# Attention, gate and branch pools that wait by tile, laid out from two ends of SBUF

## The chip, the cores and the metric

The kernel runs on one core of a Trainium2 chip. The metric is the time on the device in microseconds. Before the change three runs took 956.02, 958.73 and 959.63 us, the median is 958.73 us.

## What is computed

One decoder block over 1024 tokens of width 1024, all in fp32:

```python
h = rms_norm(x, g_pre[l], NORM_EPS)
proj = jnp.einsum('bsd,dn->bsn', h, w_in[l])
qa, ka, va, fa, za, qb, kb, vb, zb, gates = jnp.split(proj, SPLIT_POINTS, axis=-1)
log_f = jax.nn.log_sigmoid((fa + b_forget[l]).astype(jnp.float32)).transpose(0, 2, 1)
ya = fox_attention(split_heads(qa, FOX_HEADS), split_heads(ka, FOX_HEADS),
                   split_heads(va, FOX_HEADS), log_f)
ya = merge_heads(ya) * jax.nn.silu(za)
...
yb = diff_attention(qd, kd, vd, lam)
yb = rms_norm(yb, g_subln[l], SUBLN_EPS) * (1.0 - lam_init)
yb = merge_heads(yb) * jax.nn.silu(zb)
gate_a, gate_b = jnp.split(jax.nn.sigmoid(gates), N_BRANCHES, axis=-1)
merged = (gate_a * jnp.einsum('bsw,wd->bsd', ya, w_branch[l, 0])
          + gate_b * jnp.einsum('bsw,wd->bsd', yb, w_branch[l, 1]))
y = jnp.einsum('bsd,de->bse', merged, w_out[l])
x = x + rms_norm(y, g_post[l], NORM_EPS)
```

`fox_attention` is causal softmax attention of eight heads of 64, with the running sum of `log_f` added to the scores. `diff_attention` takes the difference of two causal softmaxes for each of four heads, `softmax(q1 k1) - lam * softmax(q2 k2)`, and its q and k go through rope first.

## The kernel before, in words

Every fp32 product is made of three products of a high and a low part (hi·hi, hi·lo, lo·hi). So a weight block is loaded (`raw`), its high part cast (`hi`) and its low part subtracted (`lo`); all three tiles come from `wpool`, two buffers each, in all stages.

The stages follow one another, each in pools of its own, and the bytes of a closed pool are used again by pools opened later:

1. The V stage (L119–222) normalizes x, transposes it into `hT` and projects the values of both attentions, token block by token block (`pv`, L195). The results are spilled to DRAM (`vb_d` L203, `va_d` L211).
2. Attention (L251–645) has eight units u: 0 to 3 are the heads of the differential attention, 4 to 7 pairs of heads of the other. `unit_proj` projects keys (`pk`) and queries (`pq`) in two halves c of 24 matmuls each (`project`, L246). For u below 4 each half goes through `rope` (L280): ACT copies it out of PSUM (L283), four DMAs on the SP queue swap its rows (`sw`, L287), DVE and POOL multiply by cosine and sine (L288, L289), DVE adds (L290), and `stack` makes the parts TA, TB, KA and KB (L295–298). `unit_attn` loads the unit's values (`V`, L495), builds swapped copies `X0`/`X1` of the queries by DMA (L407), and works row by row: scores (`S`, L421 and L422), their minimum on DVE (L423), exponential on ACT (L428), transposes (L450) and products with V (L474), evacuation to `y_d` (L523, L555). The projections of the next unit, of the z columns (`pz`, spilled to `z_d`) and the combinations of `hT` (`t_d`, L373) are fillers between rows. Pools: `qk` (TA, TB, KA, KB, X, V), `pp` (score rows P and small work tiles such as the lambda inputs `lt`, L570), `ptp`, `stg`, and in PSUM `pj`, `sps`, `tps2`, `yps`. `big`, opened before the V stage, holds the tables and later `cb` and is closed at L647.
3. The gates (L654–821). `h_load` (L790) loads the combined right operands T6, T5, T7, T4 from `t_d`, two tiles of 1 MB each, into `tpool`. `gates_plain(0)` makes the first gate block with 96 plain matmuls (`pg`, L246). `gates_pair(d)`, d from 1 to 7, makes the others by Winograd's form with seven products (`x1` to `x7`, L713): the two weight blocks `raw{d}_0`, `raw{d}_1` are loaded (L802), POOL makes the sums S1 to S4 (L677), ACT and DVE or POOL split them (`a1` to `a7`, L664, L665), DVE combines the products (`c`, L706), ACT applies the sigmoid (L775) and the gate is spilled (`g_d`, L776). `y_load` brings back the attention results (`yd0`, `yd1`, later `yf2`, `yf3`), `y_work` multiplies them by the z gates. Pools: `wx`, `tmp`, `ydp`, `tpool`, and `xps` in PSUM.
4. The branches (L824–873) work in `mpool` (`mg`, and `e0` to `e3`) over the bytes of `tpool`; the output projection follows.

A scheduler places the instructions of each engine by its own estimate of times, within the dependences, so the order on an engine is not that of the code. All DMAs named here are issued by one queue, SP, in its order; each uses one of eight semaphores in turn and waits for the DMA eight places before it.

By default a pool opened over released bytes makes its tiles wait for all users of every released pool there. With `reuse_waits="tile"` a tile waits for the users of those earlier tiles that lay on its own bytes (or in its own PSUM bank). With `side="right"` a pool is laid out from the upper end of SBUF downwards, otherwise from the lower end upwards.

Of the kernel before, what the change touches and what calls it, by code (L numbers as in the profile page):

```python
# [10 lines left out]
F32R = mybir.dt.float32r  # L11
AF = mybir.ActivationFunctionType
ALU = mybir.AluOpType
PSUM = bass.MemoryType.PSUM
DRAM = bass.MemoryType.DRAM

P = 128
# [4 lines left out]
CH = 512  # L22
# [19 lines left out]
def f32(ap):  # L42
    return ap.bitcast(F32)
# [3 lines left out]
def tile_hybrid_block(  # L47
# [18 lines left out]
    nc = tc.nc  # L66
# [41 lines left out]
    t_d = {m: [dram.tile([P, 4, CH], F32, name=f"t_d{m}_{part}") for part in range(2)]  # L108
           for m in (4, 5, 6, 7)}
# [9 lines left out]
    with ExitStack() as st:  # L119
        vw = st.enter_context(tc.tile_pool(name="vw", bufs=1))  # L120
        xp = st.enter_context(tc.tile_pool(name="xp", bufs=2))
        tps = st.enter_context(tc.tile_pool(name="tps", bufs=2, space=PSUM))
# [126 lines left out]


    with ExitStack() as st:  # L251
        qk = st.enter_context(tc.tile_pool(name="qk", bufs=2))
        pp = st.enter_context(tc.tile_pool(name="pp", bufs=6))
        ptp = st.enter_context(tc.tile_pool(name="ptp", bufs=3))
        stg = st.enter_context(tc.tile_pool(name="stg", bufs=2))
        pj = st.enter_context(tc.tile_pool(name="pj", bufs=2, space=PSUM))
        sps = st.enter_context(tc.tile_pool(name="sps", bufs=3, space=PSUM))
        tps = st.enter_context(tc.tile_pool(name="tps2", bufs=2, space=PSUM))
        yps = st.enter_context(tc.tile_pool(name="yps", bufs=1, space=PSUM))

        nc.sync.dma_start(gsub, g_subln.rearrange("o p -> p o"))
        nc.gpsimd.tensor_scalar(gsub, gsub, 1.0 - LAM_INIT, 1.0, op0=ALU.mult, op1=ALU.mult)
# [351 lines left out]
        T, tasks = unit_proj(0)  # L614
# [3 lines left out]
        for u in range(8):  # L618
# [5 lines left out]
            if u + 1 < 8:  # L624
                T, tasks = unit_proj(u + 1)
# [26 lines left out]


    gw = ExitStack()  # L654
    wx = gw.enter_context(tc.tile_pool(name="wx", bufs=2))
    tmp = gw.enter_context(tc.tile_pool(name="tmp", bufs=8))
    ydp = gw.enter_context(tc.tile_pool(name="ydp", bufs=1))
    xst = ExitStack()
    xps = xst.enter_context(tc.tile_pool(name="xps", bufs=8, space=PSUM))

    def split(dst, src, eng=nc.vector):

# [82 lines left out]


    tst = ExitStack()
    tpool = tst.enter_context(tc.tile_pool(name="tpool", bufs=1))

    yz = {}  # L750

# [26 lines left out]
    def gates_plain(d):  # L778
        for br in range(2):
            wt = load_w(f"g{br}_{d}", w_cols(GT + br * D + d * P), True, True)  # L780
            for c in range(2):
# [5 lines left out]
    h_ops = {m: [[hT[part][kh][sh][:, k, :] for k in range(4)] for part in range(2)]  # L787
             for m, (kh, sh) in hB.items()}

    def h_load():  # L790
        for m in (6, 5, 7, 4):
            ts = [tpool.tile([P, 4, CH], F32R, tag=f"T{m}{part}", name=f"T{m}{part}")
                  for part in range(2)]
            for part in range(2):
                nc.sync.dma_start(f32(ts[part]), t_d[m][part])
            h_ops[m] = [[t[:, k, :] for k in range(4)] for t in ts]

    def gates_pair(d, order):
        raw = []
# [8 lines left out]

    ORD = (1, 6, 5, 7, 2, 3, 4)
    h_load()  # L810
    gates_plain(0)
    for t in range(4):
# [8 lines left out]
    tst.close()  # L821


    mpool = gw.enter_context(tc.tile_pool(name="mpool", bufs=1))  # L824
    mg = mpool.tile([P, KT, S], F32, name="mg")
    hslot = {(kh, sh): [(hpool, f"h{part}{kh}{sh}") for part in range(2)]
             for kh in range(2) for sh in range(2)}
# [187 lines left out]
```

## Time and profile before

| what | us |
|---|---|
| median of three runs | 958.73 |
| the profiled execution | 960.13 |
| span of its trace | 958.0 |
| TensorE (PE) busy in the span | 900.7 |
| VectorE (DVE) busy | 627.2 |
| ScalarE (ACT) busy | 437.0 |
| GpSimd (POOL) busy | 489.6 |
| last matmul of the V stage begins | 110.26 |
| last matmul of attention begins | 602.05 |

A row of the timeline reads: start, duration, engine, line, operation, result<-inputs, shape and count, and in brackets how long the engine had idled before and what ended that. SPq are the issues of the DMA queue SP. A row of the windows lists for a stretch of time the busy time and count of PE, PEld (weight loads of TensorE), DVE, ACT and POOL, then the granted clock of TensorE as a share of full speed, the share of the DMA engines and the GB/s. Names leave numbers out: `swk` is the swapped half of a key chunk, whichever.

### The profile page before, as it was taken

To read this page: it belongs to the slowest core of one execution; us is meant where nothing else is said; L and a number is where in the kernel's file an instruction comes from. 1 tells how busy PE (TensorE), PEld (TensorE's weight loads), DVE (VectorE), ACT (ScalarE), POOL (GpSimd) and SP (SyncE) were. 2 spreads that over 40 slices of the span, in tenths; PEclk is the share of its full clock that TensorE was granted. 3 is DMA by queue.
4 is the path that set the end of the run, shared out by engine and by line. 5 is a ranking of instruction groups with operands and counts; after the bars stand their busy time and mean duration, and the time that the engine had idled before them with its cause. 6 is when DMAs were issued, how large, how long until landed. Compare 5 with 4: busy or idle time off the path is not lost.

```text
span 958.0 us, 13760 instructions
## 1 busy us (share of the span) xinstructions
PE 900.7 (94%) x4600; PEld 752.1 (79%) x4600; DVE 627.2 (65%) x1180; ACT 437.0 (46%) x862; POOL 489.6 (51%) x460
## 2 busy tenths in 40 slices
PE   7999989899999999999999988999999999999992
PEld 5999867787887888888878877777888768887871
DVE  7731258978768868578676478228665782559875
ACT  3521125665656574565745658323443550324331
POOL 7200035446545466464644575216655735878972
PEclk9999999999999999999999999998999989999997
DMA  9532454434334353534434350893445696210144
GB/s 314 193 110 91 142 134 114 105 80 123 97 94 138 95 155 116 154 122 130 143 123 136 103 186 28 325 377 122 139 138 172 186 370 203 73 38 1 48 150 154
DMA packets 115656, 136.95 MB, mean 143 GB/s; under 512 B 10609, under 2 KB 80241, under 8 KB 114562
## 3 DMA queue, kind: packets, MB, share of 16 engines
q1 hardware_dynamic: 115586, 136.08, 44.4%
q8 instruction: 36, 0.59, 0.3%
q14 instruction: 34, 0.28, 0.1%
HBM read 85.65 MB, written 37.81 MB: 129 GB/s over the span
## 4 chain that ended last, share of the span: by engine, by line
PE 58%; DVE 13%; POOL 8%; DMA 7%; issue 6%; ACT 5%; SPq 2%; DVEq 0%; POOLq 0%; ACTq 0%
PE x_g L713 11%; PE pv L195 9%; PE pb L848 9%; PE pz L246 7%; PE pk L246 4%; PE pq L246 3%; PE ypf L474 3%; PE pg L246 2%; PE ptf L450 2%; DMA swk<-rawk 2%; SPq L287 1%; DVE Pd L423 1%; PE ypd L474 1%; PE Sf L421 1%; DVE wo_op L890 1%
## 5 line engine op out<-in xcount | busy, mean ns | idle before, releaser
L195 PE MATMUL pv<-wvhi,hT 128*128 128x264 f32 (+2 forms) x384 | 89.3, 325 | 0.4 <-DVE hT L181 0.4
L246 PE MATMUL pk<-hT,hi_k 128*128 128x512 f32 x256 | 83.9, 401 | 4.2 <-DVE KB L298 2.4
L246 PE MATMUL pz<-hT,hi_z 128*128 128x512 f32 x256 | 85.1, 400 | 0.0
L848 PE MATMUL pb<-yT,hi_br 128*128 128x512 f32 x256 | 80.8, 398 | 1.9 <-ACT hi_br L232 1.6
L246 PE MATMUL pq<-hT,hi_q 128*128 128x512 f32 x256 | 82.3, 395 | 0.0
L713 PE MATMUL x_g<-T,a_g 128*128 128x512 f32 x336 | 79.5, 392 | 1.6 <-ACT a_g L664 1.2
L713 PE MATMUL x_o<-wo_op,a_o 128*128 128x512 f32 x336 | 77.4, 391 | 2.4 <-ACT a_o L664 1.2
L713 PEld LDWEIGHTS x_o<-wo_op,a_o 128*128 128x128 f32 x336 | 62.8, 188 | 16.9 <-ACT a_o L664 2.1
L713 PEld LDWEIGHTS x_g<-T,a_g 128*128 128x128 f32 x336 | 63.5, 190 | 15.7 <-ACT a_g L664 1.6
L195 PEld LDWEIGHTS pv<-wvhi,hT 128*128 128x128 f32 x384 | 64.6, 190 | 6.2 <-DVE hT L181 0.7
L542 POOL TENSOR_SCALAR Pf<-Pf,lf 128x1024 f32<-128x1024 f32 (+3 forms) x64 | 52.5, 824 | 30.2 <-DVE lf L430 27.4
L713 PE MATMUL x_g<-hT,a_g 128*128 128x512 f32 x252 | 62.0, 400 | 2.6 <-ACT a_g L664 2.0
L428 ACT ACTIVATE Pf<-Pf,mxf 128x1024 f32<-128x1024 f32 (+3 forms) x64 | 49.8, 778 | 32.1 <-DVE mxf L423 29.5
L428 ACT ACTIVATE Pd<-Pd,mxd 128x128 f32<-128x128 f32 (+7 forms) x64 | 49.5, 774 | 30.0 <-DVE mxd L423 28.2
L538 POOL TENSOR_TENSOR cb<-cb,trim 128x128 f32<-128x128 f32 x64 | 30.0, 470 | 62.9 <-DVE mxf L423 45.1
L195 PE MATMUL pv<-wvlo,hT 128*128 128x512 f32 (+2 forms) x192 | 61.9, 325 | 0.0
L512 POOL TENSOR_SCALAR Pd<-Pd,ld 128x128 f32<-128x128 f32 (+7 forms) x32 | 25.6, 799 | 68.8 <-DVE ld L511 38.2
L848 PEld LDWEIGHTS pb<-yT,hi_br 128*128 128x128 f32 x256 | 49.1, 193 | 13.1 <-ACT hi_br L232 2.0
L713 PEld LDWEIGHTS x_g<-hT,a_g 128*128 128x128 f32 x252 | 48.5, 193 | 13.7 <-ACT a_g L664 2.4
L246 PEld LDWEIGHTS pk<-hT,hi_k 128*128 128x128 f32 x256 | 47.6, 190 | 14.4 <-DVE KB L298 2.5
L454 DVE TENSOR_TENSOR plf<-ptf,phf 128x512 fp32r<-128x512 f32 (+1 forms) x80 | 49.6, 633 | 10.1 <-ACT phf L453 9.5
L246 PEld LDWEIGHTS pz<-hT,hi_z 128*128 128x128 f32 x256 | 47.9, 191 | 8.7
(243 smaller groups left out, 2426.6 us busy)
## 6 DMA issues: line engine op xcount, KB each, us to landing
t_d<-t SPq DMA_DIRECT2D x32, 256.0 KB, 2.2
T<-t_d SPq DMA_DIRECT2D x8, 1024.0 KB, 14.9
raw<-in_w_in_dram SPq DMA_DIRECT2D x14, 512.0 KB, 4.1
g_d<-c_g SPq DMA_DIRECT2D x21, 256.0 KB, 3.9
vb_d<-vbs SPq DMA_DIRECT2D x8, 512.0 KB
va_d<-vas SPq DMA_DIRECT2D x8, 512.0 KB, 3.8
raw_k<-in_w_in_dram SPq DMA_DIRECT2D x8, 512.0 KB, 5.3
raw_q<-in_w_in_dram SPq DMA_DIRECT2D x8, 512.0 KB
```

The costliest lines, as they stand in the source:

```text
L195: nc.tensor.matmul(ps[n], lhsT=hT[hp][k // 4][i // 4][:, k % 4, hs], rhs=wt[k][:, a:b], start=first, stop=(k == KT - 1 and hp == 1))
L246: nc.tensor.matmul(ps, lhsT=a[:, k, :], rhs=hT[h][k // 4][c][:, k % 4, :], start=(k == 0 and a is hi and h == 0), stop=(k == KT - 1 and a ...
L287: nc.sync.dma_start(sw[b * 32:(b + 1) * 32, :], raw[o * 32:(o + 1) * 32, :])
L428: nc.scalar.activation(pr[:, 0:n], pr[:, 0:n], AF.Exp, bias=mx[:, len(pcs) - 1:len(pcs)], scale=-1.0, accum_out=le)
L450: nc.tensor.transpose(pt[:, o * P:(o + 1) * P], rows[2 * g + r][:, j * P:(j + 1) * P], ident)
L454: nc.vector.tensor_tensor(pl[:, 0:n], pt[:, 0:n], ph[:, 0:n], op=ALU.subtract)
L474: nc.tensor.matmul(o, lhsT=a, rhs=b[:, src], start=(j == 0 and n == 0), stop=(odd == 1 and jj == g and n == len(prods) - 1))
L512: nc.gpsimd.tensor_scalar(p2[:, 0:n], p2[:, 0:n], l2, 1.0, op0=ALU.mult, op1=ALU.mult)
L538: nc.gpsimd.tensor_tensor(diag, diag, trim, op=ALU.add)
L542: nc.gpsimd.tensor_scalar(p1[:, 0:n], p1[:, 0:n], l1, 1.0, op0=ALU.mult, op1=ALU.mult)
L713: nc.tensor.matmul(x[m], lhsT=a[:, ai, k, :], rhs=right[m][bi][k], start=(k == 0 and n == 0), stop=(k == 3 and n == 2))
L848: nc.tensor.matmul(ps, lhsT=a[:, kk, :], rhs=yT[g][h][:, k % 2, sl], start=(k == 0 and a is hi and h == 0), stop=(k == 3 and a is lo))
```

## The change

All SBUF and PSUM pools of attention, gates and branches get `reuse_waits="tile"`. `pp`, `ptp` and `stg` of attention and `wx`, `tmp` and `ydp` of the gates move to the right end. In `h_load` all eight T tiles are made ahead of their loads, in the order 6, 4, 7, 5; the loads keep their order 6, 5, 7, 4. `wpool` is not changed. In the new layout the T tiles lie over `big` and `qk` of attention: T6 over `cb` of unit 7 and over TA of unit 6, T4 and T7 over the operands of units 6 and 7, T5 over V and X. Before, `tpool` lay over V, X, `pp`, `ptp` and `stg`.

```diff
-        qk = st.enter_context(tc.tile_pool(name="qk", bufs=2))
-        pp = st.enter_context(tc.tile_pool(name="pp", bufs=6))
-        ptp = st.enter_context(tc.tile_pool(name="ptp", bufs=3))
-        stg = st.enter_context(tc.tile_pool(name="stg", bufs=2))
-        pj = st.enter_context(tc.tile_pool(name="pj", bufs=2, space=PSUM))
...
+        qk = st.enter_context(tc.tile_pool(name="qk", bufs=2, reuse_waits="tile"))
+        pp = st.enter_context(tc.tile_pool(name="pp", bufs=6, side="right", reuse_waits="tile"))
+        ptp = st.enter_context(tc.tile_pool(name="ptp", bufs=3, side="right", reuse_waits="tile"))
+        stg = st.enter_context(tc.tile_pool(name="stg", bufs=2, side="right", reuse_waits="tile"))
+        pj = st.enter_context(tc.tile_pool(name="pj", bufs=2, space=PSUM, reuse_waits="tile"))
...
-    wx = gw.enter_context(tc.tile_pool(name="wx", bufs=2))
-    tmp = gw.enter_context(tc.tile_pool(name="tmp", bufs=8))
-    ydp = gw.enter_context(tc.tile_pool(name="ydp", bufs=1))
+    wx = gw.enter_context(tc.tile_pool(name="wx", bufs=2, side="right", reuse_waits="tile"))
+    tmp = gw.enter_context(tc.tile_pool(name="tmp", bufs=8, side="right", reuse_waits="tile"))
+    ydp = gw.enter_context(tc.tile_pool(name="ydp", bufs=1, side="right", reuse_waits="tile"))
...
-    xps = xst.enter_context(tc.tile_pool(name="xps", bufs=8, space=PSUM))
+    xps = xst.enter_context(tc.tile_pool(name="xps", bufs=8, space=PSUM, reuse_waits="tile"))
...
-    tpool = tst.enter_context(tc.tile_pool(name="tpool", bufs=1))
+    tpool = tst.enter_context(tc.tile_pool(name="tpool", bufs=1, reuse_waits="tile"))
...
     def h_load():
+
+        ts = {m: [tpool.tile([P, 4, CH], F32R, tag=f"T{m}{part}", name=f"T{m}{part}")
+                  for part in range(2)] for m in (6, 4, 7, 5)}
         for m in (6, 5, 7, 4):
-            ts = [tpool.tile([P, 4, CH], F32R, tag=f"T{m}{part}", name=f"T{m}{part}")
-                  for part in range(2)]
             for part in range(2):
-                nc.sync.dma_start(f32(ts[part]), t_d[m][part])
-            h_ops[m] = [[t[:, k, :] for k in range(4)] for t in ts]
+                nc.sync.dma_start(f32(ts[m][part]), t_d[m][part])
+            h_ops[m] = [[t[:, k, :] for k in range(4)] for t in ts[m]]
...
-    mpool = gw.enter_context(tc.tile_pool(name="mpool", bufs=1))
+    mpool = gw.enter_context(tc.tile_pool(name="mpool", bufs=1, reuse_waits="tile"))
```

The number of instructions on each engine stays; the order that the scheduler makes changes. On the SP queue at the start of attention, before (the names carry unit and half: `swk0_0` are the four swaps for the keys of unit 0, half 0; `va_d` and `vb_d` are the last spills of the V stage):

```order
50 L211 DMA va_d_97<-vas7_1116 128x1024
51 L572 DMA lt_1160<-in_lambda_q2_dram 128x64
52 L572 DMA lt_1160<-in_lambda_k2_dram 128x64
53 L495 DMA V0_1345<-vb_d_96 128x8x256
54 L495 DMA V1_1912<-vb_d_96 128x8x256
55 L228 DMA raw_q1_1514<-in_w_in_dram 128x8x128
56 L287 DMA swk0_0_1210<-rawk0_0_1208 32x512 x4
57 L287 DMA swq0_0_1255<-rawq0_0_1253 32x512 x4
58 L287 DMA swk0_1_1294<-rawk0_1_1292 32x512 x4
59 L407 DMA X0d0_0_1351<-TA0_1173 64x256 x2
60 L407 DMA X1d0_0_1354<-TB0_1174 64x256 x2
61 L287 DMA swq0_1_1333<-rawq0_1_1331 32x512 x4
```

The load of `raw_z0` follows three rows further down, as row 64. And after:

```order
50 L203 DMA vb_d_96<-vbs7_1112 128x1024
51 L228 DMA raw_k1_1401<-in_w_in_dram 128x8x128
52 L495 DMA V0_1345<-vb_d_96 128x8x256
53 L495 DMA V1_1912<-vb_d_96 128x8x256
54 L211 DMA va_d_97<-vas7_1116 128x1024
55 L287 DMA swk0_0_1210<-rawk0_0_1208 32x512 x4
56 L228 DMA raw_q1_1514<-in_w_in_dram 128x8x128
57 L228 DMA raw_z0_1850<-in_w_in_dram 128x8x128
58 L287 DMA swq0_0_1255<-rawq0_0_1253 32x512 x4
59 L287 DMA swk0_1_1294<-rawk0_1_1292 32x512 x4
60 L287 DMA swq0_1_1333<-rawq0_1_1331 32x512 x4
61 L407 DMA X0d0_0_1351<-TA0_1173 64x256 x2
```

The lambda loads `lt` have moved up among the earlier spills, V stands ahead of the last `va_d`, and `raw_z0` and all swaps of unit 0 stand ahead of its first X loads.

On PE, the rows around the first score of attention (`Sd0_0_0_0`), before (`pk1_0` are keys of unit 1) and after (`pq1_0` are its queries):

```order
698 L246 MATMUL pk1_0_1407<-hT100_92,hi_k1_1403 128x512
699 L246 MATMUL pk1_0_1407<-hT000_88,lo_k1_1404 128x512
700 L246 MATMUL pk1_0_1407<-hT000_88,hi_k1_1403 128x512
701 L421 MATMUL Sd0_0_0_0_1359<-KA0_1175,TA0_1173 128x128
702 L246 MATMUL pk1_0_1407<-hT100_92,hi_k1_1403 128x512
703 L246 MATMUL pk1_0_1407<-hT000_88,lo_k1_1404 128x512
704 L421 MATMUL Sd0_1_0_0_1368<-KB0_1176,TB0_1174 128x128
```

After:

```order
721 L246 MATMUL pq1_0_1520<-hT000_88,hi_q1_1516 128x512
722 L246 MATMUL pq1_0_1520<-hT100_92,hi_q1_1516 128x512
723 L246 MATMUL pq1_0_1520<-hT000_88,lo_q1_1517 128x512
724 L246 MATMUL pq1_0_1520<-hT000_88,hi_q1_1516 128x512
725 L421 MATMUL Sd0_0_0_0_1359<-KA0_1175,TA0_1173 128x128
726 L246 MATMUL pq1_0_1520<-hT100_92,hi_q1_1516 128x512
727 L421 MATMUL Sd0_1_0_0_1368<-KB0_1176,TB0_1174 128x128
728 L421 MATMUL Sd0_0_1_0_1381<-KA0_1175,TA0_1173 128x256
```

The first score has moved behind 24 more projection matmuls: before it follows 10 of `pk1_0`, after it follows all of `pk1_0` and 10 of `pq1_0`.

On the SP queue at the start of the gates, before (`T60` is the high part of T6, `ys7_0` an attention result of unit 7, `ox` a block of x for the output stage):

```order
289 L555 DMA y_d7_106<-ys7_2_6574 128x256
290 L555 DMA y_d7_106<-ys7_1_6759 128x256
291 L760 DMA yd0_7041<-y_d0_99 128x1024
292 L760 DMA yd0_7041<-y_d1_100 128x1024
293 L555 DMA y_d7_106<-ys7_0_6856 128x256
294 L760 DMA yd1_7044<-y_d2_101 128x1024
295 L760 DMA yd1_7044<-y_d3_102 128x1024
296 L931 DMA ox4_1_8960<-in_x_dram 128x512
297 L931 DMA ox5_1_8986<-in_x_dram 128x512
298 L795 DMA T60_6901<-t_d6_0_137 128x2048
299 L795 DMA T61_6902<-t_d6_1_138 128x2048
300 L795 DMA T50_6905<-t_d5_0_135 128x2048
```

After:

```order
293 L555 DMA y_d7_106<-ys7_1_6759 128x256
294 L796 DMA T60_6901<-t_d6_0_137 128x2048
295 L796 DMA T61_6902<-t_d6_1_138 128x2048
296 L796 DMA T50_6907<-t_d5_0_135 128x2048
297 L555 DMA y_d7_106<-ys7_0_6856 128x256
298 L796 DMA T51_6908<-t_d5_1_136 128x2048
299 L796 DMA T70_6905<-t_d7_0_139 128x2048
300 L796 DMA T71_6906<-t_d7_1_140 128x2048
301 L796 DMA T40_6903<-t_d4_0_133 128x2048
302 L796 DMA T41_6904<-t_d4_1_134 128x2048
303 L932 DMA ox4_1_8960<-in_x_dram 128x512
304 L932 DMA ox5_1_8986<-in_x_dram 128x512
```

The T loads stand ahead of the loads of `yd`, and three of them ahead of the last spill of attention.

On ACT at the end of gate pair 1, before (`a1_g2` is the first left operand of pair 2):

```order
538 L664 CAST a4_g1_7172<-raw1_1_7049 128x512
539 L775 ACTIVATE c22_g1_7128<-c22_g1_7128 128x512
540 L775 ACTIVATE c11_g1_7067<-c11_g1_7067 128x512
541 L775 ACTIVATE c12_g1_7107<-c12_g1_7107 128x512
542 L775 ACTIVATE cu2_g1_7089<-cu2_g1_7089 128x512
543 L664 CAST a1_g2_7203<-raw2_0_7199 128x512
544 L664 CAST a5_g2_7243<-S1_g2_7221 128x512
```

After:

```order
538 L664 CAST a4_g1_7172<-raw1_1_7049 128x512
539 L775 ACTIVATE c22_g1_7128<-c22_g1_7128 128x512
540 L775 ACTIVATE c11_g1_7067<-c11_g1_7067 128x512
541 L775 ACTIVATE c12_g1_7107<-c12_g1_7107 128x512
542 L664 CAST a1_g2_7203<-raw2_0_7199 128x512
543 L775 ACTIVATE cu2_g1_7089<-cu2_g1_7089 128x512
544 L664 CAST a5_g2_7243<-S1_g2_7221 128x512
```

The cast of `a1_g2` stands ahead of the sigmoid of `cu2_g1`. From gate pair 7 to the end the orders of all engines are the same in both.

More of the change, by code (lines that the diff above doesn't have):

```diff
@@ L251, in tile_hybrid_block @@
     with ExitStack() as st:
-        qk = st.enter_context(tc.tile_pool(name="qk", bufs=2))
-        pp = st.enter_context(tc.tile_pool(name="pp", bufs=6))
-        ptp = st.enter_context(tc.tile_pool(name="ptp", bufs=3))
-        stg = st.enter_context(tc.tile_pool(name="stg", bufs=2))
-        pj = st.enter_context(tc.tile_pool(name="pj", bufs=2, space=PSUM))
-        sps = st.enter_context(tc.tile_pool(name="sps", bufs=3, space=PSUM))
-        tps = st.enter_context(tc.tile_pool(name="tps2", bufs=2, space=PSUM))
-        yps = st.enter_context(tc.tile_pool(name="yps", bufs=1, space=PSUM))
+        qk = st.enter_context(tc.tile_pool(name="qk", bufs=2, reuse_waits="tile"))
[3 more added lines that the diff above has]
+        pj = st.enter_context(tc.tile_pool(name="pj", bufs=2, space=PSUM, reuse_waits="tile"))
+        sps = st.enter_context(tc.tile_pool(name="sps", bufs=3, space=PSUM, reuse_waits="tile"))
+        tps = st.enter_context(tc.tile_pool(name="tps2", bufs=2, space=PSUM, reuse_waits="tile"))
+        yps = st.enter_context(tc.tile_pool(name="yps", bufs=1, space=PSUM, reuse_waits="tile"))
         nc.sync.dma_start(gsub, g_subln.rearrange("o p -> p o"))
```

## The prediction

> **What bounds the kernel now.** First the page: how busy the engines are, then the slices, then the chain that ended last.
>
> ```profile
> PE 900.7 (94%) x4600; PEld 752.1 (79%) x4600; DVE 627.2 (65%) x1180; ACT 437.0 (46%) x862; POOL 489.6 (51%) x460
> PE   7999989899999999999999988999999999999992
> PE 58%; DVE 13%; POOL 8%; DMA 7%; issue 6%; ACT 5%; SPq 2%; DVEq 0%; POOLq 0%; ACTq 0%
> ```
>
> TensorE is busy 900.7 of 958.0 us, and no matmul is removed. A change of waits can therefore win only from the 57 us in which PE idles or runs at a low clock, and most of those lie where no pool changes: the slices of the first and the last 24 us stand at 7 and 2 tenths. So I looked at the two places where a pool is opened over bytes that were in use: the start of attention (110 us) and the start of the gates (602 us). How fast PE goes when nothing holds it, from the chain at the second place, and then the timeline of PE and the windows at the first:
>
> ```profile
> 603.23 22.07 PE pg L246 x96
> 110.39 0.63 PE L246 MATMUL pk<-hT,hi_k 128*128 128x512 f32 x2
> 117.10 0.50 PE L246 MATMUL pq<-hT,lo_q 128*128 128x512 f32 x1 [0.61 <-DVE lo_q L236]
> 134.99 0.70 PE L246 MATMUL pk<-hT,hi_k 128*128 128x512 f32 x2 [1.73 <-ACT rawk L283]
> 137.74 0.50 PE L246 MATMUL pk<-hT,lo_k 128*128 128x512 f32 x1 [2.04 <-DVE lo_k L236]
> 140.95 0.31 PE L421 MATMUL Sd<-KA,TA 128*128 128x128 f32 x1
> 132.00:136.00 4.00, 1.97 (x8) 1.02 (x6) 3.91 (x5) 1.82 (x3) 1.85 (x2) 1.00 0.00 0
> 136.00:140.00 4.00, 2.26 (x6) 1.83 (x7) 3.91 (x5) 1.82 (x3) 1.09 (x1) 0.78 0.33 82
> 168.00:200.00 32.00, 28.90 (x144) 24.43 (x145) 29.76 (x67) 19.44 (x35) 16.87 (x13) 0.95 0.42 111
> ```
>
> One 128x512 matmul costs 22.07/96 = 0.23 us. Attention opens with 96 projection matmuls of unit 0 and 10 of unit 1 before the first score at 140.95. Unbroken, 106 x 0.23 = 24.4 us after 110.39 would be 134.8; the first score is 6.2 us later than that. PE misses 4.00-1.97 and 4.00-2.26 = 3.8 us between 132 and 140, and the rest is a wait of 0.61 at 116.5 and a clock of 0.78. DVE is at 3.91 of 4 us in both windows. Why everything comes at once there is seen on the queues and in the first rows that rope gives:
>
> ```profile
> 110.58 0.33 SPq L572 DMA_DIRECT2D lt<-in_lambda_q_dram  x1
> 113.88 1.41 SPq L495 DMA_DIRECT2D V<-vb_d  x2
> 119.56 4.68 SPq L287 DMA_DIRECT2D swk<-rawk  x4
> 134.87 2.41 SPq L287 DMA_DIRECT2D swk<-rawk  x4
> 138.43 1.15 SPq L407 DMA_DIRECT2D X0d<-TA  x2
> 116.07 0.59 ACT L283 COPY rawk<-pk 128x512 f32<-128x512 f32 x1 [5.11 <-PE pk L246]
> 129.35 1.80 POOL L289 TENSOR_TENSOR swk<-swk,sinT 128x512 f32<-128x512 f32 x1 [19.12 <-DMA swk<-rawk]
> 132.37 1.48 POOL L234 TENSOR_SCALAR hi_k<-raw_k 128x1024 fp32r<-128x1024 f32 x1
> 136.47 1.22 DVE L236 TENSOR_TENSOR lo_k<-raw_k,hi_k 128x1024 fp32r<-128x1024 f32 x1
> 144.86 0.29 DVE L423 CUSTOM_DVE_ANT_0 Pd<-Sd,dmask 128x128 f32<-128x128 f32 x1
> 145.08 1.78 DVE L288 TENSOR_TENSOR rawq<-rawq,cosT 128x512 f32<-128x512 f32 x1
> ```
>
> The copy of the first projected chunk is there at 116.7 (116.07+0.59), yet its swap DMAs start at 119.56 and POOL has the swapped rows only at 129.35. Ahead of them on SP stand the four small lambda loads, which begin at 110.58, when the V stage's last reader of the bytes is done, and behind those the two loads of V at 113.88. POOL then does two rope products and only after them the high part of unit 1's key weights, so lo_k comes at 136.47 and PE stands.
>
> **Start of attention, part by part.** With waits by tile the lambda loads go out among the V stage's last spills, and the V loads no longer follow them. I put them at 109.2, behind the last vb_d and raw_k, 4.7 us earlier. Then the swaps are not held by the queue and leave at 116.7, when the copy is done: 119.56-116.7 = 2.9 us earlier. The two V loads in flight have also gone by then, so I take the landing 6 us earlier (at most 129.35 - 116.7 - 4.68 = 8, at least 2.9). hi_k of unit 1 now stands directly behind the first rope product on POOL and not behind the second. The rope product would start at 123.4 (129.35-6), and 1.80 for it, 1.48 for hi_k and 1.22 for lo_k make 127.9 for the end of lo_k, against 137.7 now. That is ahead of PE's need: by the new order pk of unit 1 begins after 96 matmuls, at 110.39 + 22.1 = 132.5. Both waits of PE, 1.73 and 2.04, then have nothing behind them.
>
> The order has 130 projection matmuls ahead of the first score where 106 stood: 110.39 + 130 x 0.23 = 140.3, plus at most the 0.6 at 116. The first score comes no earlier, but with 24 x 0.23 = 5.5 us of filler done. On DVE the whole rope of unit 0 is done before the first L423, where before the last chunk came after it: 1.78 for its cosine product and 3 x 0.69 for the add and the two subtractions of the stack:
>
> ```profile
> 134.42 0.69 DVE L296 TENSOR_TENSOR KA<-rawk,KA 64x512 fp32r<-64x512 f32 x1
> ```
>
> together 3.85 us. What is this lead worth? The filler would have had to be done anyway, so at most PE's lost 6.2. At the least it is the first row alone, about 1 us (144 instead of 144.86), if the filler was only needed where PE is idle anyway. I take 4: between 168 and 200 us DVE is busy 29.76 of 32 us and PE 28.90, so the smaller lead, DVE's 3.85, should be the one that survives. V, X and the score buffers cost nothing of their own: V is first needed by the products, well after 145.
>
> Moved past on SP, and priced: the load of z's weights, which has to wait for lo_k of unit 1 (it takes that raw buffer), stands ahead of three of the four swaps in the new order. With lo_k at 128 it holds them about as long as the copy of pq does (96 minus 24 matmuls: 110.39+16.6+0.6 = 127.6). So nothing, unless lo_k is late (a rival below). va_d's last spill goes behind V; unit 0's lo_q waits for its buffer, and the order has put pk's second chunk between, 24 x 0.23 = 5.5 us of cover; without it the wait of 0.6 us at 116 grows to some 2.
>
> **Start of the gates.**
>
> ```profile
> 602.05 0.28 PE L474 MATMUL ypf<-plf,V 128*128 128x128 f32 x1
> PE pg L246 <- DVE ys L552: 0.9, 1, 0.9
> 601.09 0.32 SPq L555 DMA_DIRECT2D y_d<-ys  x1
> 602.36 0.80 SPq L760 DMA_DIRECT2D yd<-y_d  x2
> 604.00:628.00 24.00, 24.00 (x107) 19.84 (x106) 4.01 (x5) 6.74 (x11) 5.24 (x4) 1.00 1.01 406
> 644.58 1.27 POOL L677 TENSOR_TENSOR S_g<-raw 128x512 f32<-128x512 f32 x1 [14.05 <-DMA raw<-in_w_in_dram]
> 645.11 0.63 ACT L775 ACTIVATE cu_g<-cu_g 128x512 f32<-128x512 f32 x1 [2.09 <-DVE cu_g L706]
> 645.64 0.60 ACT L664 CAST a_g<-raw 128x512 fp32r<-128x512 f32 x1
> 646.30 0.83 PE L713 MATMUL x_g<-hT,a_g 128*128 128x512 f32 x2 [1.95 <-ACT a_g L664]
> 647.82 4.63 PE L713 MATMUL x_g<-hT,a_g 128*128 128x512 f32 x10 [0.69 <-DVE a_g L665]
> 648.00:652.00 4.00, 4.00 (x10) 3.13 (x11) 4.00 (x4) 1.00 (x2) 3.37 (x3) 0.50 0.00 0
> ```
>
> The first gate matmul waits 0.9 us for the last copy out of the old banks; in the new program it has no wait. That 0.9 is the surest gain. The T loads go out behind the y_d spill of 601.09, some 1 us earlier than the yd loads that led the queue, but yd only moves behind T. Ahead of the second gate pair's weights stand the same bytes: T 8 MB, yd 2, ox 0.5, g_d 1, yf 2, together 13.5 MB at the window's 406 GB/s, 33 us of a full queue. So those weights land about 1 us earlier, no more. Their late landing (644.58) meets PE at the end of pair 1: idle 1.95+0.69 = 2.64 us, and then 10 matmuls take 4.63 where 10 x 0.23 and the last one's tail make 2.5, so 2.1 us go to the clock of 0.50. In the new ACT order the cast of a1 stands ahead of the cu activation that waited for DVE, so it can start when the first weight block has landed. I expect 1 to 1.7 us of the 2.64 to go, and the clock's 2.1 to go in about one case in three. The bounds are 0.9 and 0.9+2.64+2.1 = 5.6; I take 3.
>
> The rule that speaks to those 2.1 us: the Trainium skill ("TensorE: Matmul & The Clock Gate", "Why this matters for your kernels") asks for no PE-idle gap above about 3 us, one window of idle being what sets the clock back. By it two gaps of 1.95 and 0.69 would leave the clock alone; the row 648–652 disagrees with 0.50. By the rule the gate place would hold 3.5 us at most instead of 5.6.
>
> **The rest.** From the last gate pair on PE, ACT, DVE, POOL and SP stand in the same order as before, so the branch pool's new waits are priced at 0: the first mg load stands on SP behind the branch weights, the yT casts behind the last z work on ACT. T's landing under attention's old buffers costs nothing while T is first read 22 us into the gates, behind pg's 22.07 us.
>
> **Sum.** The profiled execution took 960.13 us, 1.4 above the median of the runs shown. 960.13 - 4 - 3 = 953.1; on the median's scale 951.7, so 952. A measurement of this kernel can tell about 0.5%, 4.8 us, from no change: faster is below 953.9, slower above 963.5.
>
> **Rivals.**
> - *Absorbed lead.* The filler done early leaves PE with less to put between the rows later. For it: PE is at 28.90 of 32 us from 168 to 200 with DVE at 29.76, so PE idles there for DVE. By the orders the lead of 24 to 30 matmuls is given back by unit 3 or 4. Or the change does not do what it says: something else than the old bytes (the copy, the queue's eighth DMA before) holds the swaps. Then 1 + 2 remain: 957.1, on the median's scale 956.
> - *Everything comes through.* 6.2 + 5.6 = 11.8: 948.3, on the median's scale 947. Against it: raw weights land only 1 us earlier.
> - *A new wait on SP* (slower). Unit 1's lo_k frees the buffer of z's weights, and that load now stands ahead of three swaps and the first X loads. If lo_k comes no earlier than now (it ends at 137.7), three swaps of 2.41 follow, X0d and X1d at 1.15 each and about 2 us of landing (as the t_d transfers' 2.2): X at 137.7 + 0.5 + 7.2 + 2.3 + 2 = 149.7, where the first X score runs at 143.2:
>
> ```profile
> 143.21 0.39 PE L422 MATMUL Sd<-KA,X0d 128*128 128x128 f32 x2
> 146.05 0.53 SPq L228 DMA_DIRECT2D raw_z<-in_w_in_dram  x1
> t_d<-t SPq DMA_DIRECT2D x32, 256.0 KB, 2.2
> ```
>
> 6.5 us later, and about 1.8 more for a clock near 0.5 after such a gap (as at 648). 960.13 + 8.3 - 3 = 965.4, on the median's scale 964. It decides from a lo_k later than about 130. Against it: hi_k was moved up on POOL, and V goes early.
>
> **Chances.** My forecast 0.42, the absorbed lead 0.30, everything 0.15, the new wait on SP 0.13. The forecast's own range is 949 to 955, from the bounds of each place. Leaving out the lower half of "everything" and most of the slow case gives 946 to 962 for 8 in 10. Faster by over 0.5%: 0.34 of the forecast's 0.42, 0.15, and 0.04 of the absorbed lead, 0.53. Slower: two thirds of the new wait and a little for places not seen, 0.11. Within: 0.36.
>
> **What would show it.** The swaps' first issue near 116.7 and POOL's first rope product near 123; no PE idle from 132 to 140; first score at 140 to 141, first L423 at 143 to 145; pg right behind the last attention matmul; PE idle before the second pair's first matmul 1.3 or less, and the clock at 648. If the last attention matmul is not about 4 us earlier than 602.05, the lead was absorbed. The prediction is wrong if the first L423 comes later than 146, if raw weights of pair 2 land later than 644.6, or if a slice after 200 us loses PE time that it had.

## The result and the profile after

Four runs of the changed kernel took 950.96 to 953.65 us, median 952.35; four of the kernel before 956.02 to 959.63, median 958.97. The ratio is 0.994, with a 95% interval from 0.9918 to 0.9962. The medians lie 6.6 us apart, and the forecast was 952. The profiled execution is the fastest of the four, 950.96 us, so it stands 9.2 us under the one before, and not 6.6.

First the page of the changed kernel, then the SP queue at the start of attention:

```profile
span 948.8 us, 13757 instructions
PE 896.9 (95%) x4600; PEld 747.2 (79%) x4600; DVE 627.2 (66%) x1180; ACT 437.2 (46%) x862; POOL 490.9 (52%) x460
```

```profile
109.69 1.00 SPq L495 DMA_DIRECT2D V<-vb_d  x2
112.02 1.29 SPq L211 DMA_DIRECT2D va_d<-vas  x1
117.26 2.52 SPq L287 DMA_DIRECT2D swk<-rawk  x4
...
128.81 0.38 SPq L228 DMA_DIRECT2D raw_z<-in_w_in_dram  x1
129.28 3.96 SPq L287 DMA_DIRECT2D swq<-rawq  x4
133.35 2.42 SPq L287 DMA_DIRECT2D swk<-rawk  x4
138.89 2.41 SPq L287 DMA_DIRECT2D swq<-rawq  x4
142.41 1.15 SPq L407 DMA_DIRECT2D X0d<-TA  x2
```

V leaves 4.2 us earlier than before and the first swaps, of keys, 2.3 us earlier. The first swaps of queries leave 5.0 us later (129.28, before 124.33). The second half's two leave 1.5 and 2.1 us earlier (133.35 and 138.89, before 134.87 and 140.96), but the first X loads, which now stand behind all of them, leave later: X0d at 142.41 where it left at 138.43. Now the other engines there (DVE, POOL, PE) and three windows:

```profile
121.77 1.23 DVE L236 TENSOR_TENSOR lo_q<-raw_q,hi_q 128x1024 fp32r<-128x1024 f32 x1 [9.70 <-DMA va_d<-vas]
127.55 1.23 DVE L236 TENSOR_TENSOR lo_k<-raw_k,hi_k 128x1024 fp32r<-128x1024 f32 x1
135.54 1.83 DVE L288 TENSOR_TENSOR rawq<-rawq,cosT 128x512 f32<-128x512 f32 x1 [6.04 <-DMA swq<-rawq]
149.09 0.29 DVE L423 CUSTOM_DVE_ANT_0 Pd<-Sd,dmask 128x128 f32<-128x128 f32 x1
```

```profile
122.61 1.54 POOL L289 TENSOR_TENSOR swk<-swk,sinT 128x512 f32<-128x512 f32 x1 [11.93 <-DMA swk<-rawk]
```

```profile
129.01 0.73 PE L246 MATMUL pq<-hT,hi_q 128*128 128x512 f32 x2 [0.68 <-ACT rawq L283]
141.72 0.50 PE L246 MATMUL pq<-hT,lo_q 128*128 128x512 f32 x1 [1.07 <-DVE lo_q L236]
143.67 0.22 PE L421 MATMUL Sd<-KA,TA 128*128 128x128 f32 x1
```

```profile
132.00:136.00 4.00, 4.00 (x20) 3.30 (x19) 0.46 (x1) 0.59 (x1) 0.46 (x1) 1.00 0.55 131
136.00:140.00 4.00, 4.00 (x19) 3.33 (x18) 3.90 (x3) 1.12 (x2) 3.98 (x3) 1.00 0.09 21
168.00:200.00 32.00, 31.15 (x165) 25.78 (x163) 24.44 (x63) 20.98 (x39) 17.66 (x14) 1.00 0.46 120
```

PE is busy without a gap from 132 to 140. The rows of attention, though, start at 149.09, 4.2 us later than before (144.86). And still attention ends earlier, as the last rows of PE in it and the first of the gates show:

```profile
597.92 0.27 PE L474 MATMUL ypf<-plf,V 128*128 128x128 f32 x1
598.03 0.68 PE L246 MATMUL pg<-hT,hi_g 128*128 128x512 f32 x2
```

From the first `pk` to the last `ypf` it took 491.66 us before (602.05-110.39) and 486.95 after (597.92-110.97), 4.7 less. This rests on one profile of each kernel; how far one profile can be trusted is seen below. The first gate matmul follows at once: 0.11 us instead of 1.18, 1.1 less. Then the second gate pair (PE, POOL, a window):

```profile
638.97 0.61 PE L713 MATMUL x_g<-hT,a_g 128*128 128x512 f32 x2
641.22 2.56 PE L713 MATMUL x_g<-hT,a_g 128*128 128x512 f32 x10 [1.63 <-DVE a_g L665]
644.97 0.50 PE L713 MATMUL x_g<-T,a_g 128*128 128x512 f32 x1 [1.19 <-ACT a_g L664]
```

```profile
639.34 1.27 POOL L677 TENSOR_TENSOR S_g<-raw 128x512 f32<-128x512 f32 x1 [14.07 <-DMA raw<-in_w_in_dram]
```

```profile
644.00:648.00 4.00, 3.03 (x13) 2.51 (x14) 3.63 (x4) 3.54 (x7) 4.00 (x4) 1.00 0.00 0
```

Pair 2 begins without a gap, but PE then idles 1.63 and 1.19 us inside it, 2.82 us where it was 2.64. What went is the low clock: 1.00 in all windows from 636 to 648. Pairs 1 and 2 together take 41.6 us (from 619.88 to 661.51) instead of 44.1. From pair 3 to the end it is 287.3 us against 288.8, with losses in pairs 6 and 7 and a gain at the first branches. The V stage took 0.6 us more. Together -0.6 + 4.7 + 1.1 + 2.5 + 1.5 = 9.2. Matmuls at a low clock count as busy: PE's busy time fell from 900.7 to 896.9, so 3.8 of the 9.2 us came out of it and not out of the 57 us that the prediction named as the only place to win, which are idle time alone.

### The profile page after: what moved, and what is told of

Same layout as the page of the kernel before. It is cut to its first block, busy times and chain, and to the rows that moved or that the text cites. A ratio compares the mean times of both kernels' runs of the same rounds, so it can differ in the third digit from the quotient of the medians.

```text
span 948.8 us, 13757 instructions
## 1 busy us (share of the span) xinstructions
PE 896.9 (95%) x4600; PEld 747.2 (79%) x4600; DVE 627.2 (66%) x1180; ACT 437.2 (46%) x862; POOL 490.9 (52%) x460
## 4 chain that ended last, share of the span: by engine, by line
PE 47%; DVE 16%; POOL 12%; DMA 10%; issue 8%; ACT 5%; SPq 2%; DVEq 0%; POOLq 0%; ACTq 0%
PE pv L195 10%; PE pb L849 9%; PE pz L246 7%; PE pk L246 5%; PE pq L246 4%; POOL S_g L677 3%; DMA T<-t_d 3%; PE ypf L474 2%; DMA raw<-in_w_in_dram 2%; PE ypd L474 2%; PE ptf L450 2%; DVE Pd L423 1%; DVE Pf L423 1%; POOL a_g L665 1%; POOL yd L770 1%
## 5 line engine op out<-in xcount | busy, mean ns | idle before, releaser
L849 PE MATMUL pb<-yT,hi_br 128*128 128x512 f32 x256 | 78.8, 390 | 0.3 <-DVE cu_g L706 0.3
L542 POOL TENSOR_SCALAR Pf<-Pf,lf 128x1024 f32<-128x1024 f32 (+3 forms) x64 | 50.5, 793 | 30.7 <-DVE lf L430 25.8
L713 PE MATMUL x_g<-hT,a_g 128*128 128x512 f32 x252 | 60.0, 391 | 2.0 <-DVE a_g L665 1.6
L849 PEld LDWEIGHTS pb<-yT,hi_br 128*128 128x128 f32 x256 | 47.8, 188 | 10.9 <-DVE cu_g L706 0.7
L246 PEld LDWEIGHTS pq<-hT,hi_q 128*128 128x128 f32 x256 | 47.6, 188 | 9.9 <-ACT rawq L283 1.1
```

The lines of the kernel that those rows point to most:

```text
L246: nc.tensor.matmul(ps, lhsT=a[:, k, :], rhs=hT[h][k // 4][c][:, k % 4, :], start=(k == 0 and a is hi and h == 0), stop=(k == KT - 1 and a ...
L542: nc.gpsimd.tensor_scalar(p1[:, 0:n], p1[:, 0:n], l1, 1.0, op0=ALU.mult, op1=ALU.mult)
L713: nc.tensor.matmul(x[m], lhsT=a[:, ai, k, :], rhs=right[m][bi][k], start=(k == 0 and n == 0), stop=(k == 3 and n == 2))
L849: nc.tensor.matmul(ps, lhsT=a[:, kk, :], rhs=yT[g][h][:, k % 2, sl], start=(k == 0 and a is hi and h == 0), stop=(k == 3 and a is lo))
```

## The experiments

My theory was: the gain of attention comes from a lead of filler on PE, set off by loads that no longer hold SP's queue; at the gates from one wait of PE and from the clock. The rivals: the rows, not the filler; the waits, not the layout; chance.

### Layout alone, waits alone

Without the edits on waits, and without those on sides:

```diff
-        pp = st.enter_context(tc.tile_pool(name="pp", bufs=6, side="right", reuse_waits="tile"))
+        pp = st.enter_context(tc.tile_pool(name="pp", bufs=6, side="right"))
```

```diff
-        pp = st.enter_context(tc.tile_pool(name="pp", bufs=6, side="right", reuse_waits="tile"))
+        pp = st.enter_context(tc.tile_pool(name="pp", bufs=6, reuse_waits="tile"))
```

(and so in every pool of the change). Expected of the first, the layout alone:

> The changed kernel with all reuse_waits="tile" taken out again; the two-ended layout and the T tiles made ahead stay. The order of every engine is that of the changed kernel; only the waits differ. Theory (the layout alone moved the lambda and V loads and with them the filler, the waits by tile are worth only the 0.9 us ahead of the first gate matmul): 953 to 954 us, attention ending 4 to 5 us earlier than before as in the changed kernel, the first gate matmul again waiting about 0.9 us for DVE. Rival (the waits by tile carry the gain): 957 to 959 us.

Measured: 954.5 us median, ratio to the kernel before 0.9956 (0.9942 to 0.9971). That is 4.0 us under the 958.54 of the kernel before in this round, a little over the 953 to 954 that I expected. Attention takes 486.8 us, as in the changed kernel. At the gates the pool's wait is back, and longer:

```profile
600.55 1.22 PE L246 MATMUL pg<-hT,hi_g 128*128 128x512 f32 x2 [2.08 <-DVE ys L552]
```

Two matmuls take 1.22 us there instead of 0.68: behind the 2.08 us of idle the granted clock is 0.57 from 600 to 604, and the 96 matmuls of `pg` take 23.5 us instead of 21.9. Expected of the second, the waits alone:

> The changed kernel with every side="right" taken out: all waits by tile, the layout from one end as before. At the start of attention SP keeps the order of before. Theory (layout carries the gain): 957.5 to 959 us, attention ending where it did before, 0.9 us won at the first gate matmul. Rival (waits by tile carry it): 952 to 954 us.

Measured: 956.72, ratio 0.9983 (0.997 to 0.9996). The lambda loads still stand where they stood, since in the layout from one end they lie on bytes that the V stage uses to its end (SP, then PE):

```profile
110.86 0.33 SPq L572 DMA_DIRECT2D lt<-in_lambda_q_dram  x1
```

```profile
601.07 0.28 PE L474 MATMUL ypf<-plf,V 128*128 128x128 f32 x1
601.18 0.67 PE L246 MATMUL pg<-hT,hi_g 128*128 128x512 f32 x2
```

That is 1.8 us less (by the interval 0.4 to 2.9). Attention took 489.6 us in this profile (601.07-111.52), 2.1 less than in the one of the kernel before, though SP has the order of before; beside the 1.1 us at the gates the total leaves under 1 us for it, so most of it is put down here to the spread of single profiles.

So the layout, which gives the lambda tile bytes that nobody used, brings attention's gain or nearly all of it; the waits by tile bring the 1.1 us at the gates.

### Only the lambda tile

```diff
-        lt = pp.tile([P, 4, 64], F32, tag="P", name="lt")
+        lt = const.tile([P, 4, 64], F32, name="lt")
```

> The kernel before with one edit: the lambda inputs lie in the constant pool, so their four loads wait for no released bytes. SP's order at the start of attention becomes that of the changed kernel (V, last va_d, swaps; first score after 24 more projections); the gates stay as before. Theory (the lambda loads waiting for the V stage's bytes in the middle of SP's queue are what cost the time there): 953.5 to 955 us, 4 to 5 us won by the end of attention and nothing after it. Rival (the lambda loads are covered; the gain comes from the other pools' waits): 957.5 to 959.5 us.

Measured: 952.43, ratio 0.9933 (0.9912 to 0.9955): 6.1 us less, and a little under the 953.5 to 955 that I expected. This one line in the kernel before is worth as much as the whole change. SP and PE:

```profile
111.45 1.00 SPq L495 DMA_DIRECT2D V<-vb_d  x2
112.49 1.59 SPq L211 DMA_DIRECT2D va_d<-vas  x1
117.55 2.52 SPq L287 DMA_DIRECT2D swk<-rawk  x4
```

```profile
597.35 0.28 PE L474 MATMUL ypf<-plf,V 128*128 128x128 f32 x1
598.54 0.73 PE L246 MATMUL pg<-hT,hi_g 128*128 128x512 f32 x2 [0.91 <-DVE ys L552]
```

Attention takes 486.1 us (from 111.26), and the wait ahead of the gates is still there. V leaves 0.19 us after the first `pk` here, 1.28 us ahead of it in the changed kernel and 3.49 us after it in the kernel before. Both versions also have the same order of projections (the first score follows 130 of them), which the scheduler makes once the lambda loads wait for nothing; this run does not tell the earlier V from that order.

### Rows early, without the lead

The va spills of the V stage get buffers of their own, so that `lo_q` of unit 0 does not wait for the last of them:

```diff
-            sa = wpool.tile([P, 8, 128], F32R, tag="wlo", name=f"vas{i}")
+            sa = xp.tile([P, 8, 128], F32R, tag="vas", name=f"vas{i}", bufs=2)
```

> The changed kernel with the V stage's va spills in two buffers of their own, so that lo_q of unit 0 does not wait for the landing of the last spill, which stands behind V's 2 MB. V is still loaded early, but the scheduler goes back to the old order of projections: the first score after about 106 projections, two rows of swaps ahead of X. Theory (it is the lead of filler on PE that survives, rows may even come later): rows start 5 us or more earlier than in the changed kernel, and yet 954 to 958 us, because the lead of filler is gone. Rival (rows count): 946 to 951 us, better than the changed kernel.

Measured: 954.7, ratio 0.9941 (0.9922 to 0.996). SP, DVE and windows:

```profile
123.60 2.41 SPq L287 DMA_DIRECT2D swq<-rawq  x4
...
132.90 2.69 SPq L407 DMA_DIRECT2D X0d<-TA  x2
```

```profile
140.64 0.29 DVE L423 CUSTOM_DVE_ANT_0 Pd<-Sd,dmask 128x128 f32<-128x128 f32 x1
```

```profile
130.00:150.00 20.00, 19.98 (x92) 15.85 (x91) 16.32 (x33) 8.98 (x22) 8.79 (x9) 1.00 0.53 128
150.00:170.00 20.00, 16.68 (x73) 12.49 (x72) 18.68 (x40) 11.78 (x24) 11.44 (x11) 0.91 0.30 70
```

The rows start 8.5 us earlier than in the changed kernel and PE has no gap until 150. From 150 to 170 it then loses 3.3 us and part of the clock, beside a DVE that is busy 18.68 of 20: I read this as PE having no filler in hand, which no run shows by itself. Attention takes 488.7 us. That lies between the two, close to the changed kernel's second profile (below), and the total, though within the 954 to 958 of the theory, could not be told from the changed kernel's. So the same pair was run once more without the stall of gate pair 2 in it (the last experiment).

### The changed kernel again

> The changed kernel once more, for a second profiled execution. Theory: what belongs to the change recurs (attention 4 to 5 us shorter, 1.1 us won ahead of the first gate matmul, pair 2 starting 2 us earlier but pairs 1 and 2 together only some 0.5 us shorter than in a kernel of the old gate order without a clock drop); what the clock did in the first profile at gate pair 7 and at the first branches does not. About 952 us. Rival: the 2 to 4 us at the branches are there again, and belong to the change.

Measured: 952.58, ratio 0.9948 (0.9931 to 0.9965). Attention 488.2 us, 1.3 more than in the first profile of the same program: so large is the spread of one execution there. The first gate matmul again follows at 0.11 us, pairs 1 and 2 take 41.8. At the branches the idle is back and the low clock is not (its first matmul comes at 764.19):

```profile
764.00:768.00 4.00, 2.64 (x9) 1.50 (x10) 4.00 (x3) 4.00 (x6) 3.04 (x1) 1.00 1.00 359
768.00:772.00 4.00, 4.00 (x20) 3.29 (x19) 4.00 (x5) 1.99 (x3) 2.56 (x1) 1.00 1.05 397
```

In the kernel before the same stretch was at

```profile
768.00:772.00 4.00, 2.92 (x7) 1.58 (x8) 4.00 (x4) 4.00 (x6) 3.04 (x1) 0.71 1.04 388
772.00:776.00 4.00, 4.00 (x11) 3.03 (x11) 4.00 (x4) 2.19 (x3) 2.37 (x1) 0.50 1.04 380
```

So of the two gains at the branches one (the idle) was chance: of all 13 profiles eleven have it, at 1.55 to 1.64 us, and two don't. The other (2.3 us of clock) is discussed at the end.

### Lambda tile and waits by tile, one-ended layout

The edits of "waits alone" and "only the lambda tile" together:

> The kernel before with the lambda inputs in the constant pool and all waits by tile, the layout from one end: the two causes found so far, without the two-ended layout. Theory: 4.7 to 5.6 us from attention and 1.1 us at the first gate matmul, 951 to 953 us, no different from the changed kernel. Rival (the two-ended layout itself is worth something, by T going ahead of yd): 954 to 955 us.

Measured: 953.25, ratio 0.9952 (0.9931 to 0.9972): not to be told from the changed kernel. Attention 486.2 us, first gate matmul without a wait, pairs 1 and 2 42.4 us. No gain of the two-ended layout itself is seen beyond the lambda tile's bytes.

### Weights of pair 2 ahead of yf

Two operands of pair 1 go into the slots of hT that yf takes later. So yf can't be loaded before pair 1 is done, and the weights' buffers come free earlier:

```diff
-            t = pool.tile([P, 2, 4, P], F32R, tag=tag, name=f"a{m}_{nm}")
+            if nm == "g1" and m in (3, 4):
+                t = hpool.tile([P, 4, CH], F32R, tag=f"h{m - 3}01", name=f"a{m}_{nm}")
+                t = t[:, 0:2].rearrange("p a (b c) -> p a b c", c=P)
+            else:
+                t = pool.tile([P, 2, 4, P], F32R, tag=tag, name=f"a{m}_{nm}")
```

In the changed kernel:

> The changed kernel with the operands a3 and a4 of gate pair 1 in the two hT slots that yf takes later, so that the 2 MB of yf are loaded behind the weights of pair 2 and not ahead of them, and those weights' buffers come free earlier. Theory (pair 2's weights land late because T, yd and yf stand ahead of them; PE waits about 2.8 us in pair 2 for that): the waits in pair 2 go, pairs 1 and 2 take 39 to 40 us instead of 41.6, and 949 to 951 us. Rival (something else than the landing holds pair 2, or the wait only moves to pair 3 or to yf's users): 952 to 954 us.

Measured: 948.42, ratio 0.9908 (0.9888 to 0.9928), under the 949 to 951 expected. First the weights of pair 2 on SP in the changed kernel, where they stand behind yf, then SP and PE of this run (the lines are four further down in the code):

```profile
628.70 3.53 SPq L803 DMA_DIRECT2D raw<-in_w_in_dram  x2
```

```profile
622.66 0.38 SPq L807 DMA_DIRECT2D raw<-in_w_in_dram  x1
...
626.50 0.38 SPq L807 DMA_DIRECT2D raw<-in_w_in_dram  x1
...
635.72 3.04 SPq L764 DMA_DIRECT2D yf<-y_d  x3
```

```profile
638.24 2.88 PE L717 MATMUL x_g<-hT,a_g 128*128 128x512 f32 x12
640.96 8.37 PE L717 MATMUL x_g<-T,a_g 128*128 128x512 f32 x36
```

Pair 2 runs without a gap; pairs 1 and 2 take 38.2 us. So it was the late landing of these weights that held pair 2. Whether yf's 2 MB ahead of them or the buffers that came free late did it was not taken apart: the edit moves both. In the kernel with lambda tile and waits by tile:

> The kernel with lambda inputs in the constant pool and waits by tile in the layout from one end, and a3 and a4 of pair 1 in yf's slots. Theory: the three gains add, 4.7 to 5.6 + 1.1 + 2 to 3, 948 to 951 us. Rival: 952 to 954 us, as the kernel without the last edit.

Measured: 945.7, ratio 0.9887 (0.9863 to 0.9911), under the 948 to 951 expected. Pairs 1 and 2 take 38.1 us, and attention 483.9 in that execution, the shortest of all.

### The three together on one chip

> The changed kernel with both edits: a3 and a4 of pair 1 in yf's slots, and the va spills in buffers of their own. Beside the kernel with the first edit alone it sets rows that start 8 us earlier against a lead of 24 projection matmuls, without the stall in gate pair 2 between them and the end. Theory (the lead of filler is worth as much as the rows' earlier start or more): no faster than that kernel, within 2 us of it or slower. Rival (rows decide): 3 us faster or more.

> The changed kernel with a3 and a4 of pair 1 in yf's slots, again, on the chip of the run beside it: 948 to 949 us, pairs 1 and 2 of the gates 38.2 us.

> The layout from one end with waits by tile, lambda inputs in the constant pool, a3 and a4 of pair 1 in yf's slots, again: 945 to 948 us. If it stays 2 us or more under the changed kernel with the last edit alone, the two-ended layout costs something; theory: within 2 us of it, since attention and gates are the same steps.

Measured: 947.55 (ratio 0.9871, 0.9845 to 0.9898), 947.21 (0.9882, 0.9852 to 0.9913) and 946.85 (0.987, 0.9845 to 0.9895). The three can't be told apart: rows that start at 140.15 instead of 148.85 bring nothing over the lead of filler, and the lead brings nothing over them. The shortest median of the first time, 945.7, isn't one of a better layout: attention took 486.3 us in the repeat. The versions with this edit took 945.7 to 948.4 us, 4 to 7 us under the 952.58 of the changed kernel in the round before; which of them is best can't be told.

## Why the prediction was right, and where it was not

The total and the sign held: 952.35 against 952, with attention's start as the larger part and the gates' as the smaller. How they came about was right in the cause (the lambda loads on SP's queue and the wait at the first gate) and wrong in several steps, so part of the agreement is luck.

- *Start of attention, size.* Taken 4, measured 4.7 in the first profile and 3.4 in the second (491.66-488.21), against one profile of before. The size is right.
- *Its first steps.* Swaps at 117.26 (forecast 116.7), POOL's product at 122.61 (123.4), lo_k ending at 128.78 (127.9), no idle of PE from 132 to 140. Right.
- *"First score at 140 to 141, first L423 at 143 to 145."* Wrong: 143.67 and 149.09, beyond the 146 that I had named as proof against me. The step that failed is the one from the rope to the rows: "On DVE the whole rope of unit 0 is done before the first L423". I counted that as a lead and never summed what it puts ahead of L423. The queries' projection stands behind pk's second chunk, so its swaps leave 5.0 us later than before and DVE idles 6.04 us for them (row 135.54 above). From there it works with no gap of more than about 0.1 us up to 149.09. The first score is later than forecast mostly because the V stage ended 0.6 us later and PE waited 0.23, 0.68 and 1.07 us, the last for a low part that DVE made. I had also let lo_q wait some 2 us at worst for "va_d's last spill", covered. In the chain of waits of the changed kernel that spill is the longest piece:

```profile
112.02 9.63 DMA va_d<-vas
```

 The page of before has 3.8 us for such a spill. Behind V's 2 MB it took 9.6. PE was covered as I said, for its first matmul with this lo_q has no wait of its own:

```profile
123.06 0.50 PE L246 MATMUL pq<-hT,lo_q 128*128 128x512 f32 x1
```

 So I take the spill to act through the order: with buffers of its own ("rows early") the scheduler put the queries ahead again, and the rows began at 140.64.
- *"The smaller lead, DVE's 3.85, should be the one that survives."* Wrong. The 3.85 us of rope were done ahead, but the first L423 came 4.2 us later for it, so DVE had no lead. What PE had gained can be counted: 30 us after its first `pk` it had begun 105 matmuls before and 122 after, all projections of 0.23 us at the full clock, so I estimate 17 x 0.23 = 3.9 us. The reason that I gave for the size was wrong, and that DVE's 3.85 is so near is luck.
- *"With waits by tile the lambda loads go out."* Wrong: with waits by tile alone they go out at 110.86. The layout moved them.
- *The new wait on SP.* raw_z leaves at 128.81, directly behind lo_k, and its issue ends at 129.19. The copy that the next swaps need was done at 128.97 (128.38+0.59):

```profile
128.38 0.59 ACT L283 COPY rawq<-pq 128x512 f32<-128x512 f32 x1 [0.93 <-PE pq L246]
```

 So raw_z held them by 0.2 us and no more: nearly nothing, as argued. By my own reckoning it would have decided from 130 on; it was closer than its 13% suggested.
- *Start of the gates.* The 0.9 came out as 1.1. Pair 2's weights landed 41.3 us after the first `pg`, as before (644.58-603.23 and 639.34-598.03), so 1.1 us earlier seen from the end of attention: forecast 1. The sign "PE idle before the second pair's first matmul 1.3 or less" came true to the letter, since there is none. But "1 to 1.7 us of the 2.64 to go" failed: with the cast of a1 out of the way, PE waits inside the pair for a low part from DVE (1.63) and then for a cast on ACT (1.19), 2.82 us in all. The gain is the clock, which I gave one case in three. It stayed at 1.00 in the windows of pair 2 in all three profiles with the new ACT order (changed kernel twice, layout alone: pairs 1 and 2 in 41.6 to 41.8 us), and fell in all five with the old (before, waits alone, lambda tile, rows early, lambda tile with waits: 42.1 to 44.1 us). That the order of the casts decides it is not shown: no run changed it alone.
- *The rest at 0.* From pair 3 to the end: 288.8 us before, 287.3 and 287.7 in the changed kernel, 287.3 to 290.9 in those of the first round that differ from it in waits or order. No part of the change is seen in it.
- *"If a slice after 200 us loses PE time that it had."* This sign against the forecast came too, by the windows from 200 to 240 us, before and after:

```profile
200.00:240.00 40.00, 38.12 (x207) 31.67 (x207) 31.66 (x77) 24.99 (x54) 18.80 (x16) 1.00 0.36 97
200.00:240.00 40.00, 36.88 (x196) 31.42 (x196) 35.02 (x78) 25.17 (x54) 19.25 (x18) 0.96 0.39 105
```

 PE loses 1.24 us there and part of the clock, beside a DVE that is busier. So the lead was eaten into for a while, as the rival "absorbed lead" has it; at the end of attention 4.7 us (3.4 in the second profile) were left all the same.

PE did not keep the 6.2 us that it had lost, or the 5.5 that the 24 matmuls stand for, since the new order has waits of its own (0.23, 0.68 and 1.07 us): 3.9 was what it was ahead. What stays open is why about that much is left at the end of attention. The kernel with early rows and no lead of filler ahead of the first score had begun 133 matmuls after 30 us, and yet attention took 488.7 us in it. No run had both the lead and early rows.

## What to carry to other kernels

Before reworking the waits of whole pools, look for the few instructions on the queue's chain that wait for released bytes: here four small loads with a tile of 1 KB per partition, moved to bytes that no earlier pool had used, were worth as much as the whole change. When a scheduler places the instructions, such an edit acts through the order that it makes; measure layout and waits apart. On an engine that is busy 95% of the time, work done ahead of need on that engine could not be told here from a chain that starts earlier on another.

## What the runs showed of the hardware that I had not expected

A low clock of TensorE came after waits of about 2 us, and in these profiles it went with how they were cut. The kernel with only the lambda tile changed has gaps of 1.95 and 0.32 us at gate pair 2 and these windows:

```profile
640.00:644.00 4.00, 2.10 (x5) 1.25 (x6) 2.80 (x3) 2.82 (x6) 3.87 (x3) 0.74 0.52 199
644.00:648.00 4.00, 4.00 (x17) 3.23 (x16) 4.00 (x4) 2.01 (x4) 3.42 (x3) 0.83 0.00 0
```

All five profiles with the old order of the casts have a gap of 1.95 us there, four of them a second one of 0.32 to 0.69 us close behind it, and each has a window at 0.50 to 0.74. Gaps of 1.63 to 1.81 and 1.19 us with 2.6 us of matmuls between them left it at 1.00, three times of three. One gap of 2.08 us ahead of `pg` (layout alone) was followed by 0.57. The Trainium skill ("TensorE: Matmul & The Clock Gate", "Why this matters for your kernels") has the clock set back by gaps above about 3 us; six profiles here disagree, with gaps of 1.95 and 2.08 us. Pairs 1 and 2 took 42.1 to 44.1 us with the low clock and 41.6 to 41.8 without.

At the first branches idle of 1.55 to 1.64 us came in eleven profiles. In eight of them the first 40 matmuls behind it took 13.3 to 13.7 us, in three 10.9 to 11.0; the kernel before has 0.50 there and the changed kernel's second profile 1.00, with the same order of instructions. What decides it was not tried.
